# Keeping split weight tiles in HBM: a hybrid attention / gMLP / RWKV-7 layer on one core

## The chip, the cores and the metric

One core of a Trainium2 chip runs the whole layer in one launch. The metric is the device time of one execution in microseconds (us), the median of the runs. Engines are called TensorE (PE), VectorE (DVE), ScalarE (ACT), GpSimd (POOL) and SyncE (SP); SP only issues DMAs here.

## The reference, cut to what matters

One layer on x of 2048 frames by 1024 channels, in float32:

```python
h = rmsnorm(x, pre_g) * (1 + scale) + shift          # scale, shift, gate from c @ w_ada
q_lat, kv_lat, k_rope, gm_in, rw_in, z, g_logit = split_last(h @ w_in, IN_SPLITS)
y_mla = mla_mixer(...)      # (rmsnorm(q_lat) @ w_uq), (rmsnorm(kv_lat) @ w_ukv), block-causal attention
y_gm  = gmlp_mixer(...)     # u * (W_s v + b) in blocks of 128 frames
y_rw  = rwkv7_mixer(...)    # data-dependent decay, delta-rule matrix state over time
branches = stack([y_mla, y_gm, y_rw]) * silu(z)
proj   = einsum('bsnw,nwd->bsnd', branches, w_br)    # three 512 x 1024 matrices
merged = sum(proj * sigmoid(g_logit), axis=2)
x = x + gate * rmsnorm(merged @ w_out, post_g)       # w_out is 1024 x 1024
```

w_in is 1024 x 7712. It, w_br and w_out are applied to every frame.

## The kernel before

**Tiling and stages.** The frames are worked through in four super-blocks s of 512 frames. A first stage makes the projections of super-block 0. Then, for each s, `wkv(s)` runs the RWKV recurrence and `attention(s, ...)` the attention; gemms of the same and the next super-block (gates, projections, branch products, the output product of the one before) fill TensorE between their steps. `finish` closes the last super-block. In `wkv`, each of four head pairs needs a triangular inverse (`inverses`): a chain of small VectorE operations on X and tx, whose input comes through the DMAs md and mb, and whose result goes out and comes back through xd and xtb. Then `advance` and `states` carry the matrix state (UV, QG, S, Y).

**Products in two halves.** Each float32 operand of a large product is split into a rounded half and the rest, both of type fp32r, and `mm3` sums three matmuls: high by high, high by low, low by high. A weight tile is 512 rows by 128 columns, 256 KB, held as 128 partitions of 512 values. `wgran` makes one: SP loads it raw (wr), ScalarE copies it into wh with rounding, and POOL or VectorE subtracts to get wl (`split` takes the engine with the shorter modelled backlog). Twelve matmuls use a tile. Each of the three tags wr, wh and wl has three buffers. There are 162 different tiles (120 of w_in, 2 with the rotary key's columns, 24 of w_br, 16 of w_out); every super-block loads and splits each of them, 648 times in all. The query, key and value weights of the attention are split the same way in `mla_units`, in tiles of 128 x 256 or 128 x 128 (wuq, wuqh, wuql).

**What sets the order.** Python generators, one for each strand of work, are stepped by a small planner (`Pace`) that keeps modelled times of all engines and takes the strand whose next TensorE step is ready first; its formulas of durations are the "old model". TensorE's order is fixed by this. `pace.forget(h, l)` lets the planner treat weights as ready. The framework orders the other engines, SP among them, by the order of the code and priorities: `tc.high_priority(offset=100)` puts a load of weights ahead by that much. Each engine works its instructions off in its order, so a DMA that waits on SP holds up those behind it. SP's DMAs take eight semaphores in turn (DMAHW0 to 7), and an issue waits for the DMA that last used its own.

**Names.** hh and hl are the halves of h (transposed), brh and brl those of a branch, pd the psum of the gemms, pst, pss and pso those of the strands. gt is a gate or branch tile of 128 x 512 on its way to HBM (gate_d, part_d), p a partial sum coming back. Nearly every instruction is recorded from one helper line, 121, so groups are told apart by their tiles.

Of the kernel before, what the change touches and what calls it, by code (L numbers as in the profile page):

```python
# [21 lines left out]
P = 128  # L22
# [282 lines left out]
def trunk(ctx, tc, io, out):  # L305
# [231 lines left out]
            e = V if pace.backlog("Pool") + 1.25 > pace.backlog("DVE") + .6 + BIAS else G  # L537
        e.tensor_tensor(out=lo, in0=src, in1=hi.bitcast(F32), op=ALU.subtract)

    def wgran(src):  # L540

        raw = wp.tile([P, 4, P], F32, tag="wr", name="wr", bufs=WRB)
        with tc.high_priority(offset=100):
            SY.dma_start(raw, src.rearrange("(k p) c -> p k c", p=P))
        h = wp.tile([P, 4, P], F32R, tag="wh", name="wh", bufs=WHB)
        l = wp.tile([P, 4, P], F32R, tag="wl", name="wl", bufs=WHB)
        split(h, l, raw)
        return h, l

    def mm3(o, lh, ll, rh, rl, start, stop):  # L550
        PE.matmul(o, lh, rh, start=start, stop=False)
        PE.matmul(o, lh, rl, start=False, stop=False)
        PE.matmul(o, ll, rh, start=False, stop=stop)

    def gemm(w, c0, rhs, nk=KD, r0=0):

        yield (RD, *rhs[0])
        pace.lock = pace.cur
        o = pd()
        for kg in range(nk // 4):  # L560
            pace.early = EAR
            h, l = wgran(w[r0 + kg * 512:r0 + (kg + 1) * 512, c0:c0 + P])
            pace.early = 0.0
            pace.forget(h, l)
            for k in range(4):
                kk = kg * 4 + k
                rh, rl = rhs[kk]
                yield (rh, rl)
                mm3(o, h[:, k, :], l[:, k, :], rh, rl, kk == 0, kk == nk - 1)
        pace.lock = None  # L570
        return o
# [136 lines left out]
    def mla_units(s, pl):  # L708
        st = {}
        ts_ = slice(s * SB, (s + 1) * SB)  # L710

        def lng():
            return pl.tile([P, 512], F32, tag="lng", name="lng", bufs=4)

        def parts(x, hi, lo):
            A.activation(hi, x, AF.Copy)
            split_lo(lo, x, hi)
            return hi, lo

        def wparts():  # L720
            return [pl.tile([P, 2, P], F32R, tag=n, name=n, bufs=2) for n in ("wuqh", "wuql")]

        def weights(w):
            return parts(w, *wparts())

        def first():
            yield ()
            st["trig"] = trig_of(s, pl)

        def lat(i):  # L730
            o = yield from gemm(w_in, O_Q + i * P, hT)
            x = st[i] = lng()
            A.activation(x, o, AF.Copy)
            sq = st["s", i] = mt(pl, "sq")
            A.activation(sq, o, AF.Square)

        def norms():

            yield (RT, *(st["s", i] for i in range(3)))
            o = pt()  # L740
            for j in range(4):
                for c, ids in ((0, (0, 1)), (1, (2,))):
                    for i in ids:
                        PE.matmul(o[:, c * 4 + j:c * 4 + j + 1], st["s", i][:, j * P:(j + 1) * P], ones[:, 0:1],
                                  start=i == ids[0], stop=i == ids[-1])
            ms = sm.tile([P, 8], F32, tag="mss", name="mss")
            V.tensor_scalar(ms[:, 0:4], o[:, 0:4], 1.0 / 256, None, op0=ALU.mult)
            V.tensor_scalar(ms[:, 4:8], o[:, 4:8], 1.0 / 128, None, op0=ALU.mult)
            rs = sm.tile([P, 8], F32, tag="mrs", name="mrs")
            rstd_of(rs, ms, 1.0, EPS, 8)  # L750
            for c, ids, vec in ((0, (0, 1), "mla_q_norm"), (1, (2,), "mla_kv_norm")):
                dg = mt(pl, "dg")
                for j in range(4):
                    V.tensor_scalar(dg[:, j * P:(j + 1) * P], ident, rs[:, c * 4 + j:c * 4 + j + 1], None, op0=ALU.mult)
                yield (RT, dg)
                o = pt()
                PE.matmul(o, ones, dg, start=True, stop=True)
                for n, i in enumerate(ids):
                    V.scalar_tensor_tensor(st[i], st[i], col[vec][:, n:n + 1], o, op0=ALU.mult, op1=ALU.mult)
                    st[i] = parts(st[i], *(pl.tile([P, 512], F32R, tag=n, name=n, bufs=3) for n in ("lh", "ll")))  # L760

        def rope_key():
            yield (RD, *hT[0])
            pace.lock = pace.cur
            o = pd()
            for kg in range(2):
                pace.early = EAR
                raw = wp.tile([P, 4, P], F32, tag="wr", name="wr", bufs=WRB)
                SY.dma_start(raw[:, :, 0:96], w_in[kg * 512:(kg + 1) * 512, O_KR - 64:O_KR + 32].rearrange("(k p) c -> p k c", p=P))
                G.tensor_copy(raw[:, :, 96:112], raw[:, :, 80:96])  # L770
                G.tensor_copy(raw[:, :, 112:128], raw[:, :, 64:80])
                h = wp.tile([P, 4, P], F32R, tag="wh", name="wh", bufs=WHB)
                l = wp.tile([P, 4, P], F32R, tag="wl", name="wl", bufs=WHB)
                split(h, l, raw)
                pace.early = 0.0
                pace.forget(h, l)
                for k in range(4):
                    rh, rl = hT[kg * 4 + k]
                    yield (rh, rl)
                    mm3(o, h[:, k, :], l[:, k, :], rh, rl, kg + k == 0, kg * 4 + k == 7)  # L780
            pace.lock = None
            kp, t2 = mt(pl, "kp"), mt(pl, "t2")
            rope(kp[64:96], o, st["trig"], kp[64:96], t2[64:96])
            SY.dma_start(kp_d[s], kp[64:96])

        def query(h):
            wuq = pl.tile([P, 2, P], F32, tag="wuq", name="wuq", bufs=2)
            SY.dma_start(wuq[:, :, 0:96], io["mla_w_uq"][0, :, h * 96:(h + 1) * 96].rearrange("(i p) c -> p i c", p=P))
            G.tensor_copy(wuq[:, :, 96:112], wuq[:, :, 80:96])
            G.tensor_copy(wuq[:, :, 112:128], wuq[:, :, 64:80])  # L790
            wh, wl = weights(wuq)
            pace.forget(wuq, wh, wl)
            yield (RT, *st[0], *st[1])
            o = pt()
            for i in range(2):
                mm3(o, wh[:, i, :], wl[:, i, :], *st[i], i == 0, i == 1)
            q, t2 = mt(pl, "q"), mt(pl, "t2")
            A.activation(q[0:64], o[0:64], AF.Copy)
            rope(q[64:96], o, st["trig"], q[64:96], t2[64:96])
            SY.dma_start(q_d[s][h], q[0:96])  # L800

        def keys(hp):
            raw = pl.tile([P, 2, P], F32, tag="wuq", name="wk", bufs=2)
            w = raw[:, 0]
            src = io["mla_w_ukv"][0, :, hp * 256:(hp + 1) * 256].rearrange("p (h c) -> p h c", h=2)
            SY.dma_start(w.rearrange("p (h c) -> p h c", h=2), src[:, :, 0:64])
            wh, wl = wparts()
            parts(w, wh[:, 0], wl[:, 0])
            wl = wl[:, 0]
            pace.forget(raw, wh)  # L810
            yield (RT, *st[2])
            o = pt()
            mm3(o, wh[:, 0], wl, *st[2], True, True)
            k = mt(pl, "k")
            A.activation(k, o, AF.Copy)
            SY.dma_start(k_d[s][2 * hp:2 * hp + 2].rearrange("h d t -> (h d) t"), k)

        def values():
            src = io["mla_w_ukv"][0].rearrange("p (h c) -> p h c", h=8)
            w = []  # L820
            for i in range(2):
                raw = pl.tile([P, 2, P], F32, tag="wuq", name="wv", bufs=2)
                SY.dma_start(raw.rearrange("p a (h c) -> p (a h) c", h=2), src[:, i * 4:(i + 1) * 4, 64:128])
                w.append([x.rearrange("p a b -> p (a b)") for x in weights(raw)])
            for j in range(4):
                yield (RT, *w[0], *w[1], *st[2])
                o = pt()
                for i in range(2):
                    mm3(o[:, i * 256:(i + 1) * 256], *(x[:, j * P:(j + 1) * P] for x in st[2]), *w[i], True, True)
                v = mt(pl, "vv")  # L830
                A.activation(v, o, AF.Copy)
                SY.dma_start(v_d[s][j * P:(j + 1) * P, :], v)

        return ([first] + [lambda i=i: lat(i) for i in range(3)] + [norms, rope_key]
                + [lambda h=h: query(h) for h in range(8)] + [lambda h=h: keys(h) for h in range(4)] + [values])


# [879 lines left out]
```

## Time and profile before

| | |
|---|---|
| runs | 3216.32, 3217.26, 3221.55 us; median 3217.26 |
| profiled execution | 3224.98 us; span 3223.0, granted TensorE clock 0.955 |
| TensorE busy | 92% of the span |
| VectorE, ScalarE, POOL busy | 60%, 46%, 37% |
| DMA | 432.73 MB, mean 134 GB/s; 46.7% of 16 engines' span on SP's queue |
| HBM | 328.61 MB read, 100.93 MB written |

Busy time is the union of an engine's instructions. In a group's row stand engine, operation, out<-in, shapes and count, then busy time and mean ns of one, then the idle time just before them and what ended it. A row of waits gives who waited for what: us in total, times, the longest. A row of the chain gives start and length in us. A row of a stage gives from:to, its length, busy us and count for TensorE, its weight loads, VectorE, ScalarE and POOL, then the granted clock, the DMA engines' mean busy share and GB/s; asked for one tile, it holds only the engines that touch that tile.

### The profile page before, as it was taken

The page shows a single profiled execution, that of the slowest core. Times are in us where ns is not written, and L with a number is a line of the kernel's source. Part 1 is how long each engine was busy: PE and PEld are TensorE (multiplying, and loading weights), DVE is VectorE, ACT ScalarE, POOL GpSimd, SP SyncE. Part 2 cuts the span into 40 slices and gives each one's busy share as a digit, 9 for nine tenths or more (in the row PEclk, how much of TensorE's full clock was granted, in tenths as well). Part 3 has the DMA queues.
Part 4 walks back from the last instruction along what each step waited for, and adds up shares of the span by engine and source line. Part 5 has one row for each costly group of instructions (what it writes and reads, how often), then busy time and mean ns, then how long its engine had stood idle before and what let it go on. Part 6 is the DMA issues. An engine that isn't in the chain of part 4 may idle for free. (4 is left out here: it accounts for less than half of the span.)

```text
span 3223.0 us, 48041 instructions
## 1 busy us (share of the span) xinstructions
PE 2969.3 (92%) x16156; PEld 2415.6 (75%) x16156; DVE 1923.3 (60%) x4657; ACT 1483.6 (46%) x3330; POOL 1202.0 (37%) x1129
## 2 busy tenths in 40 slices
PE   5898989899989989989998998999898899899998
PEld 4677767778767768878777776887786677688876
DVE  7437674564576745466376664557637676566653
ACT  4343333544433426554433434566544344477743
POOL 3343333434434333343533333224334343333324
PEclk8899999999999999999998998999999899899999
DMA  7443333744543566444553466444344436533345
GB/s 254 114 131 96 82 82 102 211 127 132 165 120 99 153 181 169 135 135 124 147 153 89 124 181 171 115 116 136 101 143 133 123 98 171 167 105 103 88 128 166
DMA packets 594115, 432.73 MB, mean 134 GB/s; under 512 B 143216, under 2 KB 489420, under 8 KB 593868
## 3 DMA queue, kind: packets, MB, share of 16 engines
q1 hardware_dynamic: 593696, 429.62, 46.7%
q8 instruction: 127, 2.08, 0.3%
q14 instruction: 120, 0.98, 0.1%
q10 hardware_dynamic: 172, 0.05, 0.0%
HBM read 328.61 MB, written 100.93 MB: 133 GB/s over the span
## 5 line engine op out<-in xcount | busy, mean ns | idle before, releaser
L121 POOL TENSOR_TENSOR wl<-wr,wh 128x512 fp32r<-128x512 f32 x517 | 681.5, 1320 | 1174.8 <-ACT wh L121 1099.2
L121 PE MATMUL pd<-hh,wh 128*128 128x512 f32 x1952 | 818.8, 419 | 4.9 <-ACT hh L121 3.0
L121 PE MATMUL pd<-hh,wl 128*128 128x512 f32 x1952 | 778.3, 399 | 4.9 <-DVE wl L121 4.9
L121 PE MATMUL pd<-hl,wh 128*128 128x512 f32 x1952 | 778.5, 399 | 3.6 <-POOL hl L121 3.1
L121 ACT ACTIVATE wh<-wr 128x512 fp32r<-128x512 f32 x648 | 406.6, 629 | 795.2 <-PE pd L121 443.6
L121 PEld LDWEIGHTS pd<-hh,wh 128*128 128x128 f32 x1952 | 376.9, 193 | 88.2 <-issue 6.1
L121 PEld LDWEIGHTS pd<-hh,wl 128*128 128x128 f32 x1952 | 375.2, 192 | 89.3 <-DVE wl L121 5.3
L121 PEld LDWEIGHTS pd<-hl,wh 128*128 128x128 f32 x1952 | 377.3, 193 | 70.3 <-POOL hl L121 4.2
L121 DVE TENSOR_TENSOR pw<-pst,ph 128x512 fp32r<-128x512 f32 (+2 forms) x352 | 196.4, 567 | 215.9 <-ACT ph L121 213.6
L121 PE MATMUL pd<-brh,wh 128*128 128x512 f32 x576 | 257.3, 447 | 24.3 <-DVE lastp L121 12.0
L121 ACT ACTIVATE ph<-pst 128x512 fp32r<-128x512 f32 (+2 forms) x352 | 171.4, 496 | 166.7 <-PE pst L121 133.2
L121 PE MATMUL pd<-brh,wl 128*128 128x512 f32 x576 | 236.6, 411 | 0.9 <-POOL wl L121 0.6
L121 PE MATMUL pd<-brl,wh 128*128 128x512 f32 x576 | 236.4, 410 | 0.0
L121 DVE TENSOR_SCALAR_CACHE_REDUCE p<-pss 128x512 f32<-128x512 f32 (+2 forms) x320 | 191.7, 606 | 48.1 <-PE pss L121 44.5
L121 ACT ACTIVATE p<-p,nm 128x512 f32<-128x512 f32 (+3 forms) x288 | 189.5, 660 | 58.6 <-DVE nm L121 58.3
L121 PE MATMUL pst<-consts,p 128*128 128x128 f32 x1088 | 162.6, 274 | 7.0 <-DVE pw L121 2.9
L121 PEld LDWEIGHTS pd<-brh,wh 128*128 128x128 f32 x576 | 115.2, 200 | 63.4 <-issue 14.1
L121 PE MATMUL pso<-ph,v 128*128 128x256 f32 x576 | 153.6, 288 | 0.1
L121 PE MATMUL pso<-pw,v 128*128 128x256 f32 x576 | 147.7, 284 | 4.2 <-DVE pw L121 3.9
L121 PEld LDWEIGHTS pst<-consts,p 128*128 128x128 f32 x1088 | 128.7, 141 | 25.2 <-DVE pw L121 4.6
L121 DVE TENSOR_TENSOR wl<-wr,wh 128x512 fp32r<-128x512 f32 x131 | 104.4, 800 | 66.8 <-ACT wh L121 58.8
L121 PE MATMUL pss<-kh,qh 96*128 96x512 f32 (+2 forms) x320 | 131.1, 410 | 12.0 <-ACT kh L121 7.9
(296 smaller groups left out, 5216.0 us busy)
## 6 DMA issues: line engine op xcount, KB each, us to landing
wr<-in_w_in SPq DMA_DIRECT2D x480, 256.0 KB
wr<-in_w_br SPq DMA_DIRECT2D x96, 256.0 KB
gate_d<-gt SPq DMA_DIRECT2D x64, 256.0 KB
part_d<-gt SPq DMA_DIRECT2D x64, 256.0 KB
p<-part_d SPq DMA_DIRECT2D x64, 256.0 KB
wr<-in_w_out SPq DMA_DIRECT2D x64, 256.0 KB
x<-in_x SPq DMA_DIRECT2D x56, 256.0 KB
gt<-gate_d SPq DMA_DIRECT2D x56, 256.0 KB
```

The lines of the kernel that those rows point to most:

```text
L121: r = f(*a, **k)
```

## The change

A dictionary `kept` maps each weight tile to two tiles in HBM. At the first use of a weight tile it is loaded raw and split as before, and then `keep` stores both halves by two DMAs on SP. At each later use `again` loads the two halves straight into fp32r tiles, two DMAs at high priority; ScalarE, POOL and VectorE do nothing for it. The halves loaded again rotate through the buffers of all three tags, nine buffers in all, so that a load takes the buffer of a half four or five tiles back. The attention's small weights go the same way, and the four key tiles are loaded as two.

```diff
+    kept = {}
+
+    def keep(key, h, l):
+
+        kept[key] = [dr.tile(list(x.shape), F32, name="kept") for x in (h, l)]
+        for d, x in zip(kept[key], (h, l)):
+            SY.dma_start(d, x.bitcast(F32))
+
+    def again(key, h, l):
+
+        with tc.high_priority(offset=100):
+            for d, x in zip(kept[key], (h, l)):
+                SY.dma_start(x.bitcast(F32), d)
+
+    turns = [0]
+
+    def wgran(key, fill):
+
+        if key in kept:
+            tags = [("wr", "wh"), ("wl", "wr"), ("wh", "wl")][turns[0] % 3]
+            turns[0] += 1
+            h, l = (wp.tile([P, 4, P], F32R, tag=g, name="wh" if n == 0 else "wl", bufs=WHB) for n, g in enumerate(tags))
+            again(key, h, l)
+            return h, l
         raw = wp.tile([P, 4, P], F32, tag="wr", name="wr", bufs=WRB)
         with tc.high_priority(offset=100):
-            SY.dma_start(raw, src.rearrange("(k p) c -> p k c", p=P))
+            fill(raw)
         h = wp.tile([P, 4, P], F32R, tag="wh", name="wh", bufs=WHB)
         l = wp.tile([P, 4, P], F32R, tag="wl", name="wl", bufs=WHB)
         split(h, l, raw)
+        keep(key, h, l)
         return h, l
...
-        def weights(w):
-            return parts(w, *wparts())
+        def weights(key, fill):
+            hl = wparts()
+            if key in kept:
+                again(key, *hl)
+                return hl
+            w = pl.tile([P, 2, P], F32, tag="wuq", name="wuq", bufs=2)
+            fill(w)
+            parts(w, *hl)
+            keep(key, *hl)
+            return hl
```

`gemm`, `rope_key`, `query`, `keys` and `values` now hand `wgran` or `weights` a key and a function that fills the raw tile.

Counts in the order of each program, before and after:

| | before | after |
|---|---|---|
| ScalarE wh<-wr | 648 | 162 |
| POOL wl<-wr,wh | 517 | 99 |
| VectorE wl<-wr,wh | 131 | 63 |
| SP raw loads wr | 648 | 162 |
| SP stores kept<-wh, kept<-wl | 0 | 162 and 162 |
| SP loads wh<-kept, wl<-kept | 0 | 486 and 486 |
| SP DMAs in all | 1998 | 2860 |

POOL, around the first masks m21 of super-block 2's recurrence, before:

```order
L121 TENSOR_TENSOR r_15507<-r_15507,k_15508 128x512
L121 TENSOR_TENSOR bkb_15676<-bk_15675,E_15651 128x1024
L121 TENSOR_TENSOR wl_15928<-wr_15925,wh_15927 128x512
L121 TENSOR_TENSOR wl_15967<-wr_15964,wh_15966 128x512
L121 TENSOR_TENSOR m21_16288<-abc_15777,consts_86 128x8x64 x2
L121 TENSOR_SCALAR rkb_15912<-consts_86,vcol_92 128x128
L121 TENSOR_TENSOR wl_15985<-wr_15982,wh_15984 128x512
L121 TENSOR_TENSOR wl_16011<-wr_16008,wh_16010 128x512
```

The same place after:

```order
L121 TENSOR_TENSOR r_15815<-r_15815,k_15816 128x512
L121 TENSOR_TENSOR bkb_15970<-bk_15969,E_15947 128x1024
L121 TENSOR_TENSOR m21_16554<-abc_16067,consts_86 128x8x64 x2
L121 TENSOR_SCALAR rkb_16198<-consts_86,vcol_92 128x128
L121 TENSOR_SCALAR el_16432<-E_16386 128x8
L121 TENSOR_TENSOR r_16228<-r_16228,k_16229 128x512
```

Only the recurrence's own operations are left on POOL there.

SP among the gate gemms of the attention of super-block 1, before (gt is a gate going to gate_d, vf, stg, za and ym the attention's tiles):

```order
L121 DMA gate_d11_374<-gt_12869 128x512
L121 DMA wr_13126<-in_w_in 128x4x128
L121 DMA stg_13297<-q_d1_324 96x512
L121 DMA wr_13187<-in_w_in 128x4x128
L121 DMA gate_d11_374<-gt_12981 128x512
L121 DMA wr_13226<-in_w_in 128x4x128
L121 DMA vf_13445<-v_d0_335 128x4x64
```

After:

```order
L121 DMA gate_d11_374<-gt_13219 128x512
L121 DMA wl_13412<-kept_5612 128x512
L121 DMA wh_13451<-kept_5633 128x512
L121 DMA stg_13543<-k_d1_328 64x512
L121 DMA stg_13543<-kp_d1_332 32x512
L121 DMA wl_13452<-kept_5634 128x512
L121 DMA wh_13502<-kept_5697 128x512
L121 DMA gate_d11_374<-gt_13310 128x512
```

Two loads stand for one, and the stores of gates lie between the halves.

SP in the gemms of super-block 0 ahead of its recurrence, before:

```order
L121 DMA wr_1464<-in_w_in 128x4x128
L121 DMA z_d0_343<-z2_1328 128x512
L121 DMA wr_1486<-in_w_in 128x4x128
L121 DMA wr_1504<-in_w_in 128x4x128
L121 DMA wr_1526<-in_w_in 128x4x128
L121 DMA wr_1544<-in_w_in 128x4x128
```

After:

```order
L121 DMA kept_1142<-wh_1138 128x512
L121 DMA kept_1143<-wl_1139 128x512
L121 DMA wr_1274<-in_w_in 128x4x128
L121 DMA wr_1296<-in_w_in 128x4x128
L121 DMA kept_1164<-wh_1160 128x512
L121 DMA kept_1165<-wl_1161 128x512
L121 DMA wr_1321<-in_w_in 128x4x128
L121 DMA kept_1192<-wh_1188 128x512
```

Each raw load has gained two stores on the same queue, each of which waits for the split of its tile.

More of the change, by code (lines that the diff above doesn't have):

```diff
@@ L538, in split @@
         e.tensor_tensor(out=lo, in0=src, in1=hi.bitcast(F32), op=ALU.subtract)
-    def wgran(src):
+    kept = {}
[15 more added lines that the diff above has]
+            return h, l
         raw = wp.tile([P, 4, P], F32, tag="wr", name="wr", bufs=WRB)
         with tc.high_priority(offset=100):
-            SY.dma_start(raw, src.rearrange("(k p) c -> p k c", p=P))
+            fill(raw)
         h = wp.tile([P, 4, P], F32R, tag="wh", name="wh", bufs=WHB)
@@ L561, in gemm @@
             pace.early = EAR
-            h, l = wgran(w[r0 + kg * 512:r0 + (kg + 1) * 512, c0:c0 + P])
+            src = w[r0 + kg * 512:r0 + (kg + 1) * 512, c0:c0 + P].rearrange("(k p) c -> p k c", p=P)
+            h, l = wgran((w.tensor.name, w.offset, r0 + kg * 512, c0), lambda raw: SY.dma_start(raw, src))
             pace.early = 0.0
@@ L767, in rope_key, with fill @@
                 pace.early = EAR
[L768 to L774, printed above, removed]
+                def fill(raw):
+                    SY.dma_start(raw[:, :, 0:96], w_in[kg * 512:(kg + 1) * 512, O_KR - 64:O_KR + 32].rearrange("(k p) c -> p k c", p=P))
+                    G.tensor_copy(raw[:, :, 96:112], raw[:, :, 80:96])
+                    G.tensor_copy(raw[:, :, 112:128], raw[:, :, 64:80])
+                h, l = wgran(("kr", kg), fill)
                 pace.early = 0.0
@@ L786, in query, with fill @@
         def query(h):
[L787 to L792, printed above, removed]
+            def fill(wuq):
+                SY.dma_start(wuq[:, :, 0:96], io["mla_w_uq"][0, :, h * 96:(h + 1) * 96].rearrange("(i p) c -> p i c", p=P))
+                G.tensor_copy(wuq[:, :, 96:112], wuq[:, :, 80:96])
+                G.tensor_copy(wuq[:, :, 112:128], wuq[:, :, 64:80])
+            wh, wl = weights(("q", h), fill)
+            pace.forget(wh, wl)
             yield (RT, *st[0], *st[1])
@@ L800, in query @@
             SY.dma_start(q_d[s][h], q[0:96])
+        wk = []
         def keys(hp):
[L803 to L810, printed above, removed]
+            if hp % 2 == 0:
+                src = io["mla_w_ukv"][0, :, hp * 256:(hp + 2) * 256].rearrange("p (a h c) -> p (a h) c", a=2, h=2)
+                wk[:] = weights(("k", hp), lambda raw: SY.dma_start(raw.rearrange("p a (h c) -> p (a h) c", h=2), src[:, :, 0:64]))
+                pace.forget(*wk)
             yield (RT, *st[2])
             o = pt()
-            mm3(o, wh[:, 0], wl, *st[2], True, True)
+            mm3(o, wk[0][:, hp % 2], wk[1][:, hp % 2], *st[2], True, True)
             k = mt(pl, "k")
@@ L821, in values @@
             for i in range(2):
-                raw = pl.tile([P, 2, P], F32, tag="wuq", name="wv", bufs=2)
-                SY.dma_start(raw.rearrange("p a (h c) -> p (a h) c", h=2), src[:, i * 4:(i + 1) * 4, 64:128])
-                w.append([x.rearrange("p a b -> p (a b)") for x in weights(raw)])
+                hl = weights(("v", i), lambda raw: SY.dma_start(raw.rearrange("p a (h c) -> p (a h) c", h=2), src[:, i * 4:(i + 1) * 4, 64:128]))
+                w.append([x.rearrange("p a b -> p (a b)") for x in hl])
             for j in range(4):
```

## The prediction

> **What bounds the kernel now.** I read the page's head and busy times first, then the same by stages, then the chain of work that ended last, then the waits of a stage.
>
> ```profile
> span 3223.0 us, 48041 instructions
> PE 2969.3 (92%) x16156; PEld 2415.6 (75%) x16156; DVE 1923.3 (60%) x4657; ACT 1483.6 (46%) x3330; POOL 1202.0 (37%) x1129
> ```
>
> TensorE is busy 92% of the span, so at most 253.7 us are open to any change that leaves its work alone, besides what the granted clock takes. By stages (us; busy time and count of each engine; clock; DMA share; GB/s):
>
> ```profile
> 0.00:130.00 130.00, 84.38 (x308) 62.42 (x309) 86.18 (x124) 50.98 (x97) 44.34 (x55) 0.83 0.63 202
> 130.00:230.00 100.00, 97.51 (x452) 79.25 (x451) 29.45 (x56) 36.83 (x58) 37.20 (x36) 0.98 0.46 128
> 230.00:540.00 310.00, 284.50 (x1698) 225.99 (x1697) 201.13 (x510) 111.95 (x232) 114.05 (x94) 0.95 0.35 90
> 850.00:1180.00 330.00, 304.25 (x1812) 239.60 (x1811) 220.88 (x549) 123.24 (x299) 122.92 (x102) 0.96 0.48 139
> 1610.00:1950.00 340.00, 312.12 (x1808) 246.60 (x1807) 222.85 (x551) 125.02 (x300) 121.54 (x102) 0.93 0.48 137
> 2440.00:2780.00 340.00, 311.72 (x1843) 245.53 (x1844) 226.26 (x556) 127.44 (x306) 124.67 (x104) 0.95 0.48 137
> 2780.00:3110.00 330.00, 322.47 (x1897) 280.75 (x1896) 208.60 (x598) 230.21 (x549) 107.13 (x98) 0.97 0.36 101
> ```
>
> The RWKV stages of super-blocks 1, 2 and 3 are the rows at 850, 1610 and 2440. TensorE is idle there for 25.8, 27.9 and 28.3 us, together 82; the clock takes 0.04 x 330 + 0.07 x 340 + 0.05 x 340 = 54 us more. The last attention stage (2780) is TensorE's alone: 322.47 of 330. What TensorE waits for in the first of these RWKV stages, and the chain of the last 955 us (it reaches back to 2268):
>
> ```profile
> PE pss L121 <- DVE Y L121: 5.3, 3, 2.8
> PE pd L121 <- DVE lastp L121: 4.1, 2, 2.5
> PE pss L121 <- DVE u L121: 3.2, 1, 3.2
> by line: PE pd L121 11.3%; PE pss L121 4.2%; PE pst L121 3.6%; PE pso L121 2.1%; DVE X L121 1.0%; issue 1.0%; DVE tx L121 0.7%; DVE tg L121 0.5%; DMA wr<-in_w_in 0.2%; DMA x<-in_x 0.2%; DVE y L121 0.2%; DVE Y L121 0.2%; DVE kk L121 0.2%; DV
> ```
>
> So the latency-bound part is the RWKV recurrence, and it waits for VectorE. The inverses (X, tx) alone hold 1.7% of 3223 = 55 us of a chain in which TensorE has 21.2% (683 us).
>
> **What the change takes away.** In the order of the changed program wh<-wr stands 162 times instead of 648, wl<-wr 99 times on POOL and 63 on VectorE instead of 517 and 131.
>
> ```profile
> L121 POOL TENSOR_TENSOR wl<-wr,wh 128x512 fp32r<-128x512 f32 x517 | 681.5, 1320 | 1174.8 <-ACT wh L121 1099.2
> L121 ACT ACTIVATE wh<-wr 128x512 fp32r<-128x512 f32 x648 | 406.6, 629 | 795.2 <-PE pd L121 443.6
> L121 DVE TENSOR_TENSOR wl<-wr,wh 128x512 fp32r<-128x512 f32 x131 | 104.4, 800 | 66.8 <-ACT wh L121 58.8
> ```
>
> That is 418 x 1.320 = 552 us of POOL, 486 x 0.629 = 306 us of ACT and 68 x 0.800 = 54 us of VectorE. (The small query, key and value tiles and their column copies go the same way: one answer with these.) None of the three engines is the bound, so nearly all of it costs nothing. Three things are worth time.
>
> First, POOL holds VectorE up. In an inverse of super-block 2 VectorE and POOL stand so (start, us, what):
>
> ```profile
> 1688.32 0.23 DVE L121 TENSOR_TENSOR tx<-X,mb 128x69 f32<-128x69 f32 x1
> 1688.59 1.20 DVE L121 TENSOR_TENSOR X<-X,tx 128x69 f32<-128x69 f32 x1
> 1689.82 1.20 DVE L121 TENSOR_TENSOR tx<-X,mb 128x66 f32<-128x66 f32 x1
> 1688.42 2.52 POOL L121 TENSOR_TENSOR wl<-wr,wh 128x512 fp32r<-128x512 f32 x2 [6.83 <-ACT wh L121]
> ```
>
> The operation that took 0.23 us takes 1.20 while a wl runs, twice in a row. The Trainium skill ("SBUF — State Buffer", section "SBUF: two separate sides") says the same: VectorE with two SBUF inputs and GpSimd share one exclusive pair of ports, and the loser fully blocks; the trace agrees, with the 1.20 us beside 0.23. What that costs on X, and how much POOL is wl (busy time in the stage, of these instructions alone):
>
> ```profile
> L121 DVE TENSOR_TENSOR X<-X,tx x368: 126/224/1904, 256.8 to 2709.2; 128x60 f32<-128x60 f32 x24, 128x66 f32<-128x66 f32 x16, 128x69 f32<-128x69 f32 x8, 128x63 f32<-128x63 f32 x8
> L121 DVE SCALAR_TENSOR_TENSOR X<-mb,X x192: 227/239/1255, 249.8 to 2681.5; 128x27 f32<-128x27 f32 x32, 128x26 f32<-128x26 f32 x32, 128x25 f32<-128x25 f32 x32, 128x24 f32<-128x24 f32 x32
> 2440.00:2780.00 340.00, 73.65 (x232) 0.95 0.48 137
> 2440.00:2780.00 340.00, 114.70 (x285) 55.40 (x285) 2.05 (x3) 89.67 (x68) 0.95 0.48 137
> ```
>
> 232 operations at the median of about 0.235 would be 54.5 us; they take 73.65, so 19 us are surplus in the stage (the two others hardly differ). Of POOL's 124.67 us there, 89.67 (72%) are wl: 14 us go. The chain holds 55 of the 73.65: three quarters, 10 us a stage. X is a third of VectorE's 226 us; the rest has two-input work too, but much of it reads PSUM: I add half as much, 5 us. Three stages: 45 us. Bounds: 0, if another wait stands behind each (below nothing is excluded for this term, since POOL only loses work), and 3 x 19 for X plus as much for the rest, 114, though never more than the 136 us that these stages have open.
>
> Second, the halves' own way to the end. The chain at 2510 (start, us, what):
>
> ```profile
> 2513.26 0.64 ACT wh L121
> 2513.97 1.30 POOL wl L121
> 2515.29 3.75 DMA wr<-in_w_in
> 2519.03 0.38 DVE X L121 x2
> ```
>
> A raw tile's buffer comes free only with wl, and the sync queue stands behind it. These pieces, 0.2% for the DMA (6 us) and two or three us each for wl and wh, come to some 12 us in 955. After the change no load of super-blocks 1 to 3 waits for ACT or POOL. From about 600 us on that would be 12 x 2.75 = 33; I take half, since TensorE's next wait is mostly close behind: 16, between 0 and 33.
>
> Third, the clock. Over the span it takes (1 - 0.955) x 3223 = 145 us, beside 254 idle. If 61 us of waits go, the half-clock windows near them shrink: 10, between 0 and 35 (61 x 145 / 254).
>
> **What it adds.** Stores first: 162 pairs of 256 KB, all written by super-block 0 or at the first use. The splits of wl in the dense gemms at 130:230 and in the RWKV stage behind them (the fifth and sixth numbers are VectorE's and POOL's):
>
> ```profile
> 130.00:230.00 100.00, 48.19 (x123) 23.36 (x123) 5.52 (x8) 28.62 (x22) 0.98 0.46 128
> 230.00:540.00 310.00, 103.70 (x260) 49.84 (x259) 4.57 (x6) 77.90 (x59) 0.95 0.35 90
> ```
>
> At 130:230 they are 8 + 22 = 30 pairs, 15.7 MB in 100 us: 128 GB/s become 285. The stages' shares give full rates of 90 / 0.35 = 257 to 202 / 0.63 = 321 GB/s; 128 / 0.46 = 278 is nearest, being this stage's own. At 278 the stage lengthens by 3 us, at 257 by 11, at 321 by nothing. In 230:540 it is 65 pairs, which add 110 GB/s to 90, below every rate; but md, mb, xd and xtb of the four inverses queue among them, and splits move to VectorE there. I take 12 us for super-block 0, bounds 0 and 35. The Trainium skill speaks against the change here: "DMA: Bandwidth & Descriptors", section "Anatomy of one DMA", says that most of a DMA's fixed 2 us is the receipt of the write and that it can be surprisingly long where the target is HBM, so that a buffer is held longer than the bytes need. No row here shows such a receipt by itself.
>
> Then the loads. Each later tile is two issues instead of one, 512 KB instead of 256, and each waits for TensorE's last use of a buffer 4 or 5 tiles back, where the raw tile had six tiles of lead (3 wr and 3 wh). What an issue takes, dense matmuls, the sync queue's own waits, and TensorE's for wl:
>
> ```profile
> L121 SPq DMA_DIRECT2D wr<-in_w_in x488: 367/378/3053, 24.7 to 3048.2; - x163
> 2401.77 23.81 PE pd L121 x105
> SPq L121 <- POOL wl L121: 1060.1, 424, 16.8
> SPq L121 <- POOL gt L121: 77.0, 32, 10.0
> SPq L121 <- DVE gt L121: 68.7, 38, 12.1
> PE pd L121 <- DVE wl L121: 5.2, 2, 4.9
> ```
>
> A dense tile is 12 x 0.227 = 2.72 us. From the end of tile g-4 to the start of g lie three tiles, 8.2 us. Two issues (0.76) and a landing of 3.75 need 4.5, so 3.7 us are left when nothing stands in front. The cover of this cost is that lead; where a store of gt or y in front of the load waits longer, TensorE waits for wh or wl, which it hardly does now (5.2 us). Issues on the queue go from 1,998 to 2,860; at 0.378 us that is 1081 us of 3223, no bound. I take 14 us for all of super-blocks 1 to 3, bounds 0 and 100.
>
> **The sum.** -45 - 16 - 10 + 12 + 14 = -45. The profiled execution took 3224.98 (its span and 2.0 around it): 3180. It lies 7.7 us above the median of the runs, 3217.26; so the median comes to 3172.
>
> **Rivals.**
> - *The sync queue loses its lead* (slower). The mechanism is the one above: a load behind a store that waits. It decides once the store holds the queue for more than 3.7 us. For it: the longest waits for gt are 10.0 and 12.1 us, 70 such waits in all; against: they total 145.7 us, a mean of 2.1, and the order puts the loads of four tiles ahead of them. If 50 of them cost TensorE 2 us each, 100 stands where I have 14: 3217 - 45 + 86 = 3258.
> - *The transfers are hidden and so was the rest*: VectorE's surplus goes, and the recurrence then waits for TensorE's own queue, whose order a table of durations has fixed. For it: at 850 the longest wait in sum is 5.3 us of the stage's 25.8, so the next is always near. Gains and costs cancel: 3217, within 6.
> - *The whole surplus counts*: 114 in the first term instead of 45, and 25 of clock instead of 10: -45 - 69 - 15 = -129, so 3088. For it: three quarters of X are on the chain; against: TensorE must then be busy 97% in these stages.
> - That the change does not do what it says is excluded by the counts of wh and wl in its order.
>
> **From these to the numbers.** My forecast, 3172 with its own range 3140 to 3205, has 0.48; the third rival 0.16; the second 0.10; the first 0.26. A difference under 0.2% (6 us) can't be told from none here. Faster is then 0.64, same 0.10, slower 0.26. The range 3100 to 3255 leaves out the far ends of the first and the third rival, somewhat less than half of each (0.18).
>
> **What would show it.** Right: X and tx in the stage at 2440 near 58 us instead of 73.65; POOL under 700 us; TensorE's idle time in each RWKV stage under 20 us; the attention stage of 330 us unchanged; DMA share at 130:230 near 0.9. Wrong: TensorE waits on DMA for wh or wl with tens of us in sum; the sync queue's waits for gt grow; or X gets faster and the RWKV stages do not get shorter, which would speak for the second rival.

## The result and the profile after

| | before | after |
|---|---|---|
| median of 4 runs (us) | 3216.79 (3210.19 to 3221.55) | 3143.88 (3137.15 to 3145.31) |
| ratio, 95% interval | | 0.9771, 0.9748 to 0.9793 |
| profiled execution | 3224.98; span 3223.0 | 3137.15; span 3135.3 |
| granted clock, span | 0.955 | 0.967 |

The change makes the kernel faster by 2.3%, 73 us. The forecast of 3172 lay 28 us above, and the time stands inside its own range, 3140 to 3205, near the lower end.

The page's head and busy times of the kernel after:

```profile
span 3135.3 us, 47903 instructions
PE 2929.2 (93%) x16156; PEld 2386.1 (76%) x16156; DVE 1726.8 (55%) x4574; ACT 1216.8 (39%) x2804; POOL 621.6 (20%) x622
```

POOL's work is halved. TensorE does the same 16,156 matmuls. Of the 87.7 us between the spans it saves 47.6 in idle time (253.7 to 206.1) and 40.1 in busy time (2969.3 to 2929.2). The second is about what the clock gives back: 0.033 of 3135 us are withheld, 103, instead of 145.

The costliest groups, those of the split that are left:

```profile
L121 POOL TENSOR_TENSOR wl<-wr,wh 128x512 fp32r<-128x512 f32 x99 | 130.8, 1322 | 423.9 <-ACT wh L121 303.8
L121 ACT ACTIVATE wh<-wr 128x512 fp32r<-128x512 f32 x162 | 101.5, 629 | 245.5 <-PE pd L121 83.1
```

The inverse's operation on X (smallest/median/largest ns):

```profile
L121 DVE TENSOR_TENSOR X<-X,tx x368: 153/222/1842, 283.1 to 2622.8; 128x60 f32<-128x60 f32 x24, 128x66 f32<-128x66 f32 x16, 128x69 f32<-128x69 f32 x8, 128x63 f32<-128x63 f32 x8
```

**Where the time came from.** To compare programs whose stages drift apart, I cut the spans where TensorE had done equal work: every matmul counts for the median step of its form in the kernel before, the counts are summed up in order of time, and each cut stands where the sum reaches its value of before. Each column is one execution, and where TensorE's order differs from that of before a cut is good to some 4 us. Lengths of the pieces, in us (the kernels of the last four columns are described below):

| piece of before | before | after | fills | subtractions | all on VectorE, no halves | halves, rest on VectorE |
|---|---|---|---|---|---|---|
| 0:130, projections | 130 | 122 | 120 | 120 | 125 | 126 |
| 130:230, dense gemms | 100 | 118 | 118 | 120 | 100 | 103 |
| 230:540, RWKV 0 | 310 | 309 | 311 | 314 | 296 | 291 |
| 540:850 | 310 | 308 | 315 | 316 | 305 | 308 |
| 850:1180, RWKV 1 | 330 | 316 | 307 | 316 | 316 | 308 |
| 1180:1610, attention 1 | 430 | 419 | 427 | 434 | 423 | 418 |
| 1610:1950, RWKV 2 | 340 | 320 | 315 | 340 | 324 | 301 |
| 1950:2440, attention 2 | 490 | 465 | 475 | 473 | 484 | 476 |
| 2440:2780, RWKV 3 | 340 | 324 | 328 | 362 | 322 | 317 |
| 2780:3110, attention 3 | 330 | 322 | 325 | 327 | 327 | 327 |

After, the RWKV stages of super-blocks 1 to 3 are 50 us shorter, the pieces of attention 1 to 3 44, and the dense gemms of super-block 0, with the stores, 18 us longer. The stages by busy time and count of each engine (columns as before):

```profile
122.00:240.00 118.00, 102.91 (x447) 80.78 (x446) 30.37 (x48) 33.34 (x55) 25.83 (x27) 0.96 0.86 280
857.00:1173.00 316.00, 300.21 (x1779) 238.52 (x1778) 201.63 (x541) 104.32 (x262) 64.68 (x59) 0.95 0.67 210
1173.00:1592.00 419.00, 403.48 (x2099) 333.52 (x2098) 205.31 (x559) 165.73 (x377) 72.86 (x75) 0.98 0.69 219
1592.00:1912.00 320.00, 300.24 (x1827) 236.28 (x1826) 191.38 (x556) 88.99 (x237) 39.97 (x40) 0.98 0.63 195
1912.00:2377.00 465.00, 449.46 (x2387) 379.45 (x2387) 237.35 (x621) 212.30 (x486) 87.99 (x91) 0.98 0.62 197
2377.00:2701.00 324.00, 304.46 (x1859) 239.69 (x1856) 195.83 (x565) 93.79 (x244) 39.99 (x40) 0.98 0.64 198
2701.00:3023.00 322.00, 317.64 (x1872) 277.19 (x1871) 195.55 (x577) 204.78 (x499) 79.39 (x77) 0.99 0.48 148
```

The attention pieces of super-blocks 1 and 2 before:

```profile
1180.00:1610.00 430.00, 408.02 (x2076) 336.97 (x2074) 238.29 (x579) 223.60 (x494) 172.77 (x175) 0.97 0.50 142
1950.00:2440.00 490.00, 461.60 (x2402) 386.02 (x2402) 275.76 (x672) 269.12 (x597) 178.03 (x185) 0.96 0.46 130
```

TensorE's idle time (length less busy time) falls from 82.0 to 55.1 us in the three RWKV stages, and from 57.9 to 35.4 in the three attention pieces; in the dense gemms it rises from 2.5 to 15.1.

X and tx alone in the stage of super-block 3 (232 operations before and after):

```profile
2377.00:2701.00 324.00, 53.31 (x232) 0.98 0.64 198
```

They fell from 73.65 to 53.31 us. What SP's queue waits for now (total, times, longest):

```profile
SPq L121 <- PE pd L121: 755.2, 369, 10.3
SPq L121 <- POOL gt L121: 59.7, 29, 4.8
SPq L121 <- DVE gt L121: 50.2, 37, 4.6
```

And TensorE, its longest wait in sum and its longest for a tile kept:

```profile
PE pss L121 <- DVE Y L121: 16.6, 8, 4.2
PE pst L121 <- DMA wuqh<-kept: 2.4, 2, 1.4
```

SP's issues now stand behind TensorE's last use of a buffer, but TensorE hardly waits for a half loaded again: the longest such entry is 2.4 us in sum. The waits for gt, 77.0 and 68.7 us before, fell.

### The profile page after: what moved, and what is told of

The parts are those of the page before. It is cut to its first block, busy times and chain, and to the rows that moved or that the text cites. A ratio compares the mean times of both kernels' runs of the same rounds, so it can differ in the third digit from the quotient of the medians.

```text
span 3135.3 us, 47903 instructions
## 1 busy us (share of the span) xinstructions
PE 2929.2 (93%) x16156; PEld 2386.1 (76%) x16156; DVE 1726.8 (55%) x4574; ACT 1216.8 (39%) x2804; POOL 621.6 (20%) x622
## 5 line engine op out<-in xcount | busy, mean ns | idle before, releaser
L121 POOL TENSOR_TENSOR wl<-wr,wh 128x512 fp32r<-128x512 f32 x99 | 130.8, 1322 | 423.9 <-ACT wh L121 303.8
L121 ACT ACTIVATE wh<-wr 128x512 fp32r<-128x512 f32 x162 | 101.5, 629 | 245.5 <-PE pd L121 83.1
L121 POOL TENSOR_TENSOR kl<-stg,kh 96x512 fp32r<-96x512 f32 x80 | 102.8, 1289 | 226.6 <-ACT kh L121 202.4
```

The lines of the kernel that those rows point to most:

```text
L121: r = f(*a, **k)
```

## The experiments

Each ratio is against runs of the kernel before on the same chip, with its 95% interval. "The order of before" or "of the changed kernel" means that the planner's decisions of that kernel were written down and played back, so that TensorE's strands are stepped in the same order.

**1. The order alone.** `halves_old_order` is the changed kernel in the order of before, `splits_new_order` the kernel before in the order of the changed one.

```diff
-            best, key, at = None, self.INF, 0.0
...
+            self.pos = getattr(self, "pos", -1) + 1
+            best = next(th for th in self.threads if th[3] == STEPS[self.pos])
```

> The changed kernel, with TensorE's order forced to be that of the kernel before, step by step. Before is 3216.8, changed 3143.9. Theory P (POOL's splits no longer hold VectorE up) and theory W (the halves reach their buffers without ScalarE and POOL) both expect nearly the whole gain, 3140 to 3160, since the freed engines do not depend on the planner. Theory O (the planner, which saw other backlogs, chose a better order) expects 3190 to 3215.

> The kernel before, with TensorE's order forced to be that of the changed kernel. Theories P and W expect the time of before or worse, 3210 to 3250, since the order was planned for other costs. Theory O expects 3150 to 3180.

Measured: 3133.90 us, ratio 0.9728 (0.9693 to 0.9764), and 3220.42 us, 0.9997 (0.9975 to 1.0019). The new order is worth nothing, and the halves in the old order give the gain by themselves. Several kernels below keep the old order, so that they can be compared piece by piece.

**2. POOL's subtractions put back.** `halves_pool_sub` is the changed kernel in which, for six of seven tiles loaded again, POOL subtracts the two loaded halves into a scratch tile that nothing reads: 417 operations, against 418 that the change takes from POOL. `halves_pool_fill` makes POOL as busy without two large SBUF inputs: a copy of one column and three fills.

```diff
             again(key, h, l)
+            if turns[0] % 7:
+                nc.gpsimd.tensor_tensor(out=idle_..., in0=h..., in1=l..., op=ALU.subtract)    # halves_pool_sub
```

```diff
+                nc.gpsimd.tensor_copy(idle_[:, 0:1], h[:, 0, 0:1].bitcast(F32))               # halves_pool_fill
+                nc.gpsimd.memset(idle_, 0.0)
+                nc.gpsimd.memset(idle_, 0.0)
+                nc.gpsimd.memset(idle_[:, 0:256], 0.0)
```

> The changed kernel, and for six of seven later weight tiles POOL does a subtraction of the two loaded halves into a scratch tile that nobody reads: 417 operations of the shape of wl, about 1.32 us each, at the places where the splits stood. TensorE's order is that of the changed kernel. Theory P expects 40 to 65 us of the 73 back, 3185 to 3210, with X in the recurrence stage of super-block 3 near 73 us again. Theory W expects 3145 to 3155, since no load and no matmul waits for it.

> As the kernel with the subtraction, but POOL fills the scratch tile with zeros for about as long (fills of 512, 512 and 256 columns behind a copy of one column), so that it is as busy but reads next to nothing. Theory P, in the form that the ports of reading are what VectorE waits for, expects 3143 to 3155 and X in the recurrence stage of super-block 3 under 62 us. If it is POOL's own operations that come late (m21, dg, the splits of keys), it is as slow as the subtraction, 3185 to 3210.

Measured: 3238.88 us, 1.0054 (1.0032 to 1.0077), for the subtractions; 3157.30 us, 0.9795 (0.9763 to 0.9827), for the fills. They ran on the same chip: 81.6 us lie between them. The subtractions cost more than I expected: they take back the whole gain and 0.5% more, though the copies that the change took from ScalarE stay away. What this 0.5% is made of was not separated. The span and the busy times in the page of the kernel with subtractions:

```profile
span 3238.5 us, 48694 instructions
PE 2973.0 (92%) x16156; PEld 2416.2 (75%) x16156; DVE 1818.5 (56%) x4574; ACT 1216.0 (38%) x2804; POOL 1170.4 (36%) x1039
```

its costliest POOL group:

```profile
L565 POOL TENSOR_TENSOR idle<-wh,wl 128x512 f32<-128x512 f32 x417 | 554.3, 1329 | 1117.6 <-DMA wl<-kept 1041.7
```

The span and the busy times of the kernel with fills:

```profile
span 3155.8 us, 49943 instructions
PE 2934.2 (93%) x16156; PEld 2388.4 (76%) x16156; DVE 1723.0 (55%) x4574; ACT 1216.8 (39%) x2804; POOL 1272.8 (40%) x2290
```

and its POOL groups:

```profile
L565 POOL COPY idle<-wh 128x1 f32<-128x1 f32 x417 | 91.4, 219 | 923.1 <-DMA wh<-kept 919.5
L566 POOL MEMSET idle<- 128x512 f32 x417 | 220.3, 528 | 24.7
```

The idle time at the rows' end shows that both kinds stand behind the landing of a half for about as long. POOL is busier with the fills (1272.8 us against 1170.4), yet the same 4,574 VectorE instructions take 1723.0 us beside them and 1818.5 beside the subtractions. The RWKV stage of super-block 3 with the subtractions, all engines:

```profile
2434.00:2796.00 362.00, 321.12 (x1856) 252.66 (x1856) 223.15 (x565) 93.30 (x243) 120.94 (x101) 0.93 0.57 178
```

X and tx alone:

```profile
2434.00:2796.00 362.00, 68.11 (x232) 0.93 0.57 178
```

The same stage with the fills, all engines:

```profile
2388.00:2715.00 327.00, 309.94 (x1854) 245.03 (x1853) 193.67 (x565) 93.31 (x242) 134.53 (x281) 0.96 0.63 195
```

and X and tx alone:

```profile
2388.00:2715.00 327.00, 52.41 (x232) 0.96 0.63 195
```

565 VectorE instructions take 223.15 or 193.67 us, and the stage 362 or 327. It is what POOL reads that holds VectorE up, not how long POOL is busy. Nor is it that the subtraction keeps the halves' buffers longer: SP's queue waits 3.4 us in all for the subtractions, and 87.8 us for the copies and fills of the faster kernel. The Trainium skill, "SBUF — State Buffer", section "SBUF: two separate sides", limits the lock on the shared ports in this way: a VectorE operation with two SBUF inputs meets it only against a GpSimd operation that reads SBUF. These rows agree, 52.41 us of X beside 68.11. Of the 81.6 us, 68 lie in the three RWKV stages of super-blocks 1 to 3 (9, 25 and 34 by the table).

**3. The stores alone.** `splits_and_stores` is the kernel before with the 162 pairs (and those of the attention's weights) stored and never loaded again, in the order of before.

```diff
-        if key in kept:
+        if False:
             tags = ...
```

> The kernel before in its own order, and at each weight tile's first use both halves are also stored to HBM as in the change; nothing is loaded from there, all 648 splits stay. So it prices the stores alone. My forecast put 12 us on them, bounds 0 and 35, so 3229 beside 3217. If the stores are hidden, 3217 to 3222; if the sync queue's order behind the splits is what they cost, 3235 to 3252.

Measured: 3239.85 us, 1.0068 (1.0042 to 1.0094): 22 us slower than the kernel before. By equal work the kernel is 19 us behind at 600 us and 23 us at 850, and then the gap shrinks to 2 us at 3110; but the profiled execution, 3227.03 us, is itself 13 us below its median, and that of before 8 us above its own, so the later part of the gap can't be read from this pair. 18.7 us come from 130:230, and the seven other profiled kernels with stores on SP and some low halves made on POOL show 18 to 21 there. The stage:

```profile
130.00:248.00 118.00, 104.93 (x450) 81.50 (x450) 35.54 (x61) 37.81 (x60) 31.37 (x32) 0.94 0.83 271
```

**4. A shorter lead.** `halves_lead3` lets the halves loaded again rotate through the buffers of wh and wl alone: three tiles of lead instead of 4.5. Order of the changed kernel.

```diff
-            tags = [("wr", "wh"), ("wl", "wr"), ("wh", "wl")][turns[0] % 3]
+            tags = ("wh", "wl")
```

> The changed kernel in its own order, but loaded halves rotate through the buffers of wh and wl alone, three each, so that a load waits for the tile three back (end of g-3 to start of g: 5.4 us of dense matmuls) instead of four or five. If the lead of the sync queue is a term (my forecast put 14 us on two issues and 3.75 us of landing against 8.2 us), taking a third of it away costs 30 to 80 us more, 3175 to 3225, with waits of TensorE on wh<-kept and wl<-kept. If the lead has room, 3140 to 3155.

Measured: 3161.28 us, 0.9843 (0.9815 to 0.9870), 0.7% or some 23 us above the changed kernel: less than I expected, but a cost. SP's wait for a buffer:

```profile
SPq L121 <- PE pd L121: 813.9, 394, 9.8
```

It grows from 755.2 us. The waits of TensorE that I had named hardly came: 4.5 us in all for wh<-kept and wl<-kept. So by which wait the shorter lead costs its time is not shown.

**5. ScalarE's work put back.** `halves_act_copy` adds an unread ScalarE copy of the high half for each tile loaded again, 486 of 0.63 us. `halves_act_copy_prev` copies the half loaded one tile earlier instead, to get rid of the wait for its landing.

```diff
             again(key, h, l)
+            nc.scalar.activation(idle_..., h.bitcast(F32), AF.Copy)          # halves_act_copy
```

> The changed kernel in its own order, and for each later weight tile ScalarE also copies the loaded high half into a scratch tile that nobody reads, 486 copies of some 0.63 us, where the rounding copies stood. It prices what ScalarE's relief is worth. Theory P (POOL's reads hold VectorE) expects 3143 to 3155. If ScalarE's relief is worth the 16 us of my second term, 3155 to 3165.

> The changed kernel, in its own order, with 483 unread ScalarE copies of the high half of the tile loaded before, one in place of each high half that is no longer made, so that the copy hardly waits for a landing (the copies of the half just loaded stood waiting for 492 us). Theory A (ScalarE's 306 us of work are themselves worth time, the prediction's second term): 3165 to 3180, as with those copies, 3175. Theory B (what cost 31 us there was ScalarE's queue standing behind landings): 3140 to 3155.

Measured: 3175.12 us, 0.9886 (0.9858 to 0.9914), and 3185.35 us, 0.9915 (0.9883 to 0.9948). The second was to tell occupancy from waiting and did not, since its copies stand behind landings as long as the first's. The group of the first kernel:

```profile
L564 ACT ACTIVATE idle<-wh 128x512 f32<-128x512 f32 x486 | 305.8, 629 | 494.9 <-DMA wh<-kept 492.0
```

and of the second:

```profile
L553 ACT ACTIVATE idle<-wh 128x512 f32<-128x512 f32 x485 | 305.3, 629 | 517.6 <-DMA wh<-kept 515.2
```

Both lie above all that was expected of them: 31 and 41 us above the changed kernel by the medians, 37 and 46 by the ratios. ScalarE's time alone is worth that much at most, since waiting is added to it; how much of it is the queue behind the landing stays open. What the old copies cost by standing on a half's way to TensorE is not in it, since nothing waits for these.

**6. No halves at all, no POOL.** `splits_all_vector` is the kernel before, in its own order, with all 648 subtractions on VectorE.

```diff
-        split(h, l, raw)
+        split(h, l, raw, V)
```

> The kernel before in its own order, with all 648 subtractions wl on VectorE and none on POOL. VectorE gets 517 x 0.69 = 357 us more of its own work, and POOL's 517 reads that hold it up go. Theory P, that the hold-ups were worth some 90 us of time, expects 3190 to 3225, since the added work lies partly beside other waits. If VectorE's own load is what counts, it is 60 us slower or more, over 3275.

Measured: 3131.06 us, 0.9750 (0.9721 to 0.9778). That was far below what I expected, and as fast as the change, though nothing is kept. Its busy times:

```profile
PE 2926.0 (93%) x16156; PEld 2387.6 (76%) x16156; DVE 2083.8 (66%) x5172; ACT 1487.1 (47%) x3330; POOL 545.5 (17%) x614
```

and the group of the subtractions:

```profile
L121 DVE TENSOR_TENSOR wl<-wr,wh 128x512 fp32r<-128x512 f32 x648 | 480.9, 744 | 321.9 <-ACT wh L121 307.3
```

VectorE has 160 us more to do than before (2083.8 against 1923.3): 377 us of added subtractions, less 216 us by which the rest of its work got shorter. X and tx are as fast as with the halves, 54.85 us in the stage of super-block 3 (this kernel alone would not single out POOL's reads, since a low half is also ready sooner, in 0.744 us instead of 1.320; experiment 2 does):

```profile
2372.00:2695.00 323.00, 54.85 (x232) 0.98 0.50 146
```

**7. Both together.** In the order of before: `halves_old_order_vector` makes the 162 low halves that remain on VectorE, `halves_stores_actq` issues the stores on ScalarE's queue, `halves_vector_actq` does both.

```diff
-        split(h, l, raw)
+        split(h, l, raw, V)                  # vector
         keep(key, h, l)
...
-            SY.dma_start(d, x.bitcast(F32))
+            A.dma_start(d, x.bitcast(F32))   # actq
```

> The changed kernel in the order of before, with the low half of all 162 tiles that are still split made on VectorE, so that POOL makes none. Theory (POOL's subtractions hold VectorE up, and those left stand in super-blocks 0 and 1): the kernel with all 648 subtractions on VectorE gained 37 us by the end of super-block 0, where the changed kernel gained nothing; half of that at least should come, less the 22 us of the stores that stay: 3100 to 3122 against 3134 for the halves in that order. Rival (what is lost in super-block 0 is the stores alone): 3128 to 3140.

> The changed kernel in the order of before, with the stores of the halves issued on ScalarE's queue instead of SyncE's. Theory A (the 20 us that the stores cost are SyncE's queue: a load stands behind a store that waits for its split): the queue is free of them, 3115 to 3125. Theory B (they cost by the bytes that the DMA engines move at 86% busy): nothing changes, 3128 to 3140, or more where ScalarE stands waiting for POOL's wl before it may go on, up to 3150.

> Both edits: low halves on VectorE alone and the stores on ScalarE's queue, in the order of before. If the two losses of super-block 0 are separate, the gains add: 3085 to 3115. If the stores cost by their bytes, it is as with the low halves on VectorE alone: 3100 to 3125.

Measured: 3093.61 us, 0.9606 (0.9576 to 0.9635); 3112.71 us, 0.9668 (0.9637 to 0.9699); 3105.23 us, 0.9644 (0.9613 to 0.9674). The first two beat the changed kernel and 0.9728 of the same order; the gains do not add. The first lies below its own theory's range and the second just below theory A's, both far from their rivals; the third fits both of its expectations and decides nothing. The 37 us in the first expectation are not borne out by the table, where the kernel without halves is ahead by 24 us at 850. The dense gemms of super-block 0 with the low halves on VectorE:

```profile
126.00:229.00 103.00, 98.38 (x454) 78.99 (x453) 46.71 (x81) 37.55 (x59) 9.24 (x14) 0.99 0.91 302
```

and with the stores on ScalarE's queue:

```profile
122.00:222.00 100.00, 97.80 (x454) 79.57 (x453) 32.33 (x60) 38.50 (x61) 31.42 (x31) 0.98 0.90 300
```

In about as many matmuls, these pieces take 103 and 100 us with all stores in them, at 300 GB/s, where the changed kernel needs 118 at 280. So the bytes were not what cost 18 us: the DMA engines had room. Who waits for a store to give a buffer free, in the changed kernel in the order of before:

```profile
ACT wh L121 <- DMA kept<-wh: 45.7, 25, 4.4
POOL wl L121 <- DMA kept<-wl: 42.0, 7, 10.2
```

and with the low halves on VectorE:

```profile
ACT wh L121 <- DMA kept<-wh: 19.4, 12, 2.6
DVE wl L121 <- DMA kept<-wl: 12.9, 5, 3.8
```

The split of a tile waits for the store of a half three tiles back, which stands on SP behind others that wait for POOL. A faster split or a queue of their own lets the stores leave sooner; which of the two, the queue or the buffers, does most was not separated. The Trainium skill, "DMA: Bandwidth & Descriptors", section "Anatomy of one DMA", which had spoken against the change, describes a DMA issued from GpSimd, whose completion waits for the receipt of the write. These stores were issued on SP, and no row tells how much of a wait for one is receipt.

## Why the prediction was right, and where its terms were not

**The mechanism.** It was as forecast: POOL's subtraction holds up VectorE's operations with two SBUF inputs, and the recurrence waits for VectorE. Experiment 2 shows it, and experiment 6 agrees from the other side: the reading put back costs 81.6 us more than fills do, and taking it away without any halves gives about the ratio of the change. All the signs named came but one. X and tx fell to 53.31 us (near 58 was named); POOL to 621.6 (under 700); TensorE is idle in the three RWKV stages for 15.8, 19.8 and 19.5 us (under 20); the DMA share in the dense gemms is 0.86 (near 0.9). The last attention stage was to stay at 330 and takes 322.

**First term, -45: the right size, made up of parts that were not.** The term stands for waits (it is 45 of the 61 us from which the clock term is worked out), so it is compared with idle time, and subtractions against fills is the pair that isolates it. TensorE's idle time there is 265.5 and 221.6 us, 43.9 apart; in the three RWKV stages alone it is 93.2 and 48.5, 44.7 apart. VectorE's surplus in these stages is 70.9 us: X has 39.7 of it, where 3 x 19 = 57 were read, and the rest 31.2, nearly as much as X, where half as much was taken. That the two errors nearly cancel is luck. In the change itself the idle time of these stages fell by 27 us only: the subtractions put back cost more there than those of before (93.2 us idle against 82.0), and the loads that came in are in the time after.

**Third term, -10: the step that failed.** The step from waits to clock took 10 us for 61 us of waits, 35 at most. TensorE's busy time for the same matmuls fell by 40.1 us, and between subtractions and fills by 38.8 of the 82.7 us between the spans. Over all fourteen profiles of this case TensorE's idle time goes from 188 to 266 us and its busy time from 2909 to 2973: 0.8 us of busy time for each us of idle. With 40 in place of 10 the same sum gives 3142 beside the 3143.88 measured. So near a hit is luck too, since the terms below miss one by one.

**Second, fourth and fifth terms, -16, +12 and +14: near in sum, not one by one.** They give +10. What is left of the change beside the subtractions is 82 - 73 = 9 us by the medians, but 82.7 - 87.7 = -5 by the profiled executions, so the sum is near nothing and its sign is not shown. The stores cost 22 us rather than 12 beside POOL's subtractions, inside the bounds of 0 and 35. The step behind 12 priced them by their bytes and the stage's rate. That rate was right, 280 GB/s against 278, but the stage still grew by 18 us: it was not the bytes but the wait for buffers and queue that experiment 7 takes away. There the stage grows by 3 us or by nothing, as the rates of 278 and 321 had given. Of the later loads, TensorE's waits show 2.4 us at the longest entry; that the lead matters is shown by its price (cut by a third, some 17 us by the medians, 23 by the ratios), though not by the waits that the prediction named. The halves' own way to the end looks larger than 16. With all subtractions off POOL, the halves still bring 0.9750 to 0.9606, 37 us by the medians and 46 by the ratios, with stores and loads paid; how much of that is ScalarE's copies and how much VectorE's 362 us of subtractions saved (486 x 0.744) is open. It shows above all in the RWKV stages of super-blocks 2 and 3 (28 us by the table). In the attention pieces, where the prediction named no wait and expected the last to stay, the change took 44 us, the kernel without halves only 16. Subtractions and fills hardly differ there (1234 and 1227 us in sum), so POOL's reads are not what was saved; what was is open.

**The rivals.** SP losing its lead (3258) did not come: its waits for gt fell to 59.7 and 50.2 us, where they were to grow. Hidden anyway (3217) is refuted by the ratio. The whole surplus (3088) did not come: it put 114 us on the first term, where TensorE had 82 us of idle time to give in these stages and gave 27. With POOL's last subtractions gone as well the halves reach 3093.61, near its number, but that kernel also gains in super-block 0, so it does not bear the rival out. Its 25 us for the clock were nearer than the forecast's 10.

## What to carry to other kernels

Before moving a cost to memory, look at which engine's *kind of access* hurts the critical engine. Here a change of one argument (the subtraction on VectorE, though VectorE is the engine that TensorE waits for) gave as much as storing 85 MB, and the two together gave 3.9%. An engine that is busy 37% of the span, and that TensorE hardly waits for, can still set the pace by what it reads while another engine works; compare one short operation with and without it beside. Count time won at the waits together with the clock: here each was about as large as the other. And price an added store by what its queue and its buffers make others wait for, not by its bytes alone.

## What the runs showed of the hardware

- POOL's fill of 128 x 512 in 0.53 us leaves VectorE alone (X and tx 52.41 us in the stage of super-block 3, 53.31 without fills); its subtraction of 128 x 512 in 1.29 us (median) does not (68.11).
- TensorE's busy time for the same matmuls followed its idle time, 0.8 us for 1, with granted clocks from 0.954 to 0.972. That this is cause and effect was not tested.
- A VectorE subtraction of 128 x 512 took 0.744 us on average when POOL made none, 0.800 when it made most of them.
- With stores and loads mixed, the DMA queue moved 302 GB/s over 103 us at a share of 0.91, and TensorE's dense gemms took 103 us where they had taken 100.
